# Channel products in float16 parts with column scales found on the chip

## The chip, the cores and the metric

The kernel runs on one core of a Trainium2 chip. A core has five engines with instruction queues of their own: TensorE (PE; its weight loads are listed apart as PEld), VectorE (DVE), ScalarE (ACT), GpSimd (POOL) and SyncE (SP, which here only starts transfers). Each takes its instructions in order and they wait for each other by semaphores. The metric is the device time of one execution in microseconds; less is better.

## What is computed

An encoder block for a sequence of 2048 tokens and one of 256, each token 1024 numbers in float32. One input projection feeds a short gated convolution (512 channels) and a latent attention with 8 heads; both are gated and joined by an output projection, and the result is normalised and added to the input.

```python
def _rmsnorm(x, g):
    xf = x.astype(jnp.float32)
    y = xf * lax.rsqrt(jnp.mean(xf * xf, axis=-1, keepdims=True) + NORM_EPS)
    return (y * g.astype(jnp.float32)).astype(x.dtype)

def _layer(x, norm_pre, w_in, conv_w, q_norm, w_uq, kv_norm, w_ukv, w_out, norm_post):
    hdn = _rmsnorm(x, norm_pre)
    proj = jnp.einsum('bsd,de->bse', hdn, w_in)
    u, b_gate, c_gate, z_conv, q_lat, kv_lat, k_pe, z_attn = jnp.split(proj, _split_points(), axis=-1)
    conv_out = b_gate * _short_conv(c_gate * u, conv_w) * jax.nn.silu(z_conv)
    ...
    attn_out = _attention(q_full, k_full, v) * jax.nn.silu(z_attn)
    mix = jnp.concatenate([conv_out, attn_out], axis=-1)
    out = jnp.einsum('bse,ed->bsd', mix, w_out)
    return x + _rmsnorm(out, norm_post)
```

The change is in the projection's columns u, b_gate, c_gate, z_conv and z_attn, five times 512 channels: 20 tiles of 128 channels.

## The kernel before

Float32 accuracy is made of three matmuls: each operand is cut into a rounded part hi and the rest lo, and `mm3` (L87) adds hi by hi, hi by lo and lo by hi in PSUM.

`phase1` (L103) works on the 2304 tokens as 6 chunks of 384 in two halves of three. For a chunk, `fetch_t` (L129) loads the transposed tokens into `xt` (one buffer, 1.5 MB), and `form` (L138) multiplies them by the norm's weights g_pre and cuts them into `hdn_hi` and `hdn_lo` in a rounded float32 type (F32R). `fetch_x` and `norm_x` (L144, L149) load 128 tokens at a time, and make their norms' factors (tile rc) with `rstd` (L96), a raising to the power -0.5 on GpSimd. `latents` (L176) makes the 672 columns of q_lat, kv_lat and k_pe of 128 tokens (tiles pq, pk); the weights wl are cut once. Nine such tiles make up a half.

`spread` (L166) turns a half's nine columns of factors into one row through TensorE and memory (r_s) and reads it back into all partitions (tile rb).

Then come the half's 20 tiles of channels. `load_w` (L231) fetches 512 KB of weights (tile w) and cuts them, ScalarE making whi, VectorE wlo. `etile` (L242) makes, for three chunks, 24 products each into PSUM (tile o; 72 products a tile of channels, 2880 in all), and multiplies by the tokens' row rb as it reads them: u into cu (e = 0), c_gate times cu (e = 1, with rb once more on GpSimd), b_gate into gt (e = 2), and silu of z into gt (e = 3), after which `conv` (L295) does the three taps. The last four tiles of a half (j = 4) are z_attn, stored to memory as gate. The weights of tile n + 1 are asked for just ahead of tile n.

From tile 24 on the preparation of the second phase (`Phase2.open`) is fed in between. After phase1 come the projections from the latents (L91 to L93 on k, v, q), attention with its order by hand, and the output projection. In `phase1` no order is written by hand: a scheduler places each instruction on its engine's queue by priority and expected readiness, and the queues then run in that order.

## Time and profile before

| | us |
|---|---|
| median of 3 runs (1690.73 to 1694.63) | 1692.76 |
| the profiled execution's own time | 1692.56 |
| its span | 1690.6 |
| TensorE busy in the span | 1647.5 (97%) |
| VectorE, ScalarE, GpSimd busy | 750.2, 581.6, 878.5 |

The profile is one execution. Busy time is from the start of an instruction to its recorded end; matmuls overlap each other by design, so what a matmul costs in a dense stretch is the time from its start to the next one's. The chain that ended last names 11% on TensorE, in the output projection: it reaches back only a short way, so the stages have to be read from tables by stretch and from the timeline.

### The profile page before, as it was taken

The page shows a single profiled execution, that of the slowest core. Times are in us where ns is not written, and L with a number is a line of the kernel's source. Part 1 is how long each engine was busy: PE and PEld are TensorE (multiplying, and loading weights), DVE is VectorE, ACT ScalarE, POOL GpSimd, SP SyncE. Part 2 cuts the span into 40 slices and gives each one's busy share as a digit, 9 for nine tenths or more (in the row PEclk, how much of TensorE's full clock was granted, in tenths as well). Part 3 has the DMA queues.
Part 4 walks back from the last instruction along what each step waited for, and adds up shares of the span by engine and source line. Part 5 has one row for each costly group of instructions (what it writes and reads, how often), then busy time and mean ns, then how long its engine had stood idle before and what let it go on. Part 6 is the DMA issues. An engine that isn't in the chain of part 4 may idle for free. (4 is left out here: it accounts for less than half of the span.)

```text
span 1690.6 us, 22364 instructions
## 1 busy us (share of the span) xinstructions
PE 1647.5 (97%) x8870; PEld 1115.8 (66%) x8870; DVE 750.2 (44%) x1125; ACT 581.6 (34%) x804; POOL 878.5 (52%) x637
## 2 busy tenths in 40 slices
PE   8999999999999999978999999999999999999998
PEld 8999999999999997556333333333333333378886
DVE  4333332423474222337556665666666666132122
ACT  7521111452222122411444444444444444512211
POOL 3321221033342112145788988989899898942222
PEclk9999999999999999989999999999999999999999
DMA  8921112364324116378011131113111210034443
GB/s 292 273 87 60 52 52 83 112 165 118 114 94 137 55 62 167 106 194 214 13 32 32 44 85 41 44 32 94 31 45 32 69 44 13 26 105 144 149 141 109
DMA packets 141741, 158.97 MB, mean 94 GB/s; under 512 B 33842, under 2 KB 118116, under 8 KB 141636
## 3 DMA queue, kind: packets, MB, share of 16 engines
q1 hardware_dynamic: 122916, 148.11, 29.3%
q10 hardware_dynamic: 18720, 9.44, 1.9%
q8 instruction: 69, 1.13, 0.3%
q14 instruction: 36, 0.29, 0.1%
HBM read 109.72 MB, written 41.89 MB: 90 GB/s over the span
## 5 line engine op out<-in xcount | busy, mean ns | idle before, releaser
L809 POOL TENSOR_TENSOR acc<-acc,p 128x1024 f32<-128x1024 f32 x224 | 527.9, 2357 | 60.6 <-ACT p L799 50.5
L753 DVE TENSOR_REDUCE mx<-m 128x1 f32<-128x512 f32 x512 | 337.7, 691 | 237.2 <-PE m L752 237.1
L799 ACT ACTIVATE p<-s,exps 128x1024 f32<-128x1024 f32 x256 | 271.4, 1111 | 348.2 <-PE s L794 348.2
L91 PE MATMUL o<-hdn_hi,whi 128*128 128x384 f32 x960 | 323.5, 337 | 0.0
L92 PE MATMUL o<-hdn_lo,whi 128*128 128x384 f32 x960 | 322.7, 336 | 0.0
L93 PE MATMUL o<-hdn_hi,wlo 128*128 128x384 f32 x960 | 322.6, 336 | 0.0
L789 PE MATMUL s<-q,k 128*128 128x512 f16 x1024 | 302.7, 381 | 1.0 <-ACT p L799 1.0
L920 PE MATMUL o<-p,v 128*64 128x512 f32 x1024 | 247.7, 605 | 0.0
L789 PEld LDWEIGHTS <-k 128*128 128x128 f16 x1024 | 90.7, 98 | 190.8 <-issue 101.4
L752 PE MATMUL m<-k,q 96*128 96x512 f16 x512 | 195.4, 382 | 14.4 <-DVE mx L753 8.7
L91 PEld LDWEIGHTS o<-hdn_hi,whi 128*128 128x128 f32 x960 | 180.5, 188 | 0.5
L92 PEld LDWEIGHTS o<-hdn_lo,whi 128*128 128x128 f32 x960 | 180.5, 188 | 0.0
L93 PEld LDWEIGHTS o<-hdn_hi,wlo 128*128 128x128 f32 x960 | 180.5, 188 | 0.0
L920 PEld LDWEIGHTS o<-p,v 128*64 128x64 f32 x1024 | 62.2, 136 | 127.5 <-issue 127.0
L959 PE MATMUL out<-wo,o_cut 128*128 128x512 f32 x576 | 140.4, 396 | 0.0
L959 PEld LDWEIGHTS out<-wo,o_cut 128*128 128x128 f32 x576 | 108.0, 188 | 27.7 <-issue 0.8
L948 POOL TENSOR_TENSOR o_cut<-o_raw,o_cut 128x1024 fp32r<-128x1024 f32 x17 | 40.8, 2399 | 118.3 <-ACT o_cut L945 118.3
L279 POOL TENSOR_TENSOR gt<-gt,z 128x384 f32<-128x384 f32 x24 | 28.7, 1197 | 141.1 <-ACT z L278 141.1
L236 ACT ACTIVATE whi<-w 128x1024 fp32r<-128x1024 f32 x40 | 42.2, 1058 | 172.8 <-PE o L92 159.6
L752 PEld LDWEIGHTS <-q 96*128 96x128 f16 x512 | 49.6, 97 | 63.9 <-issue 6.2
L967 DVE TENSOR_TENSOR yt<-out,g_post 128x1024 f32<-128x1024 f32 x18 | 22.0, 1224 | 150.7 <-ACT junko L966 141.7
L271 POOL TENSOR_TENSOR cu<-cu,rb 128x384 f32<-128x384 f32 (+2 forms) x28 | 27.5, 987 | 112.4 <-DVE cu L270 112.4
(230 smaller groups left out, 2016.4 us busy)
## 6 DMA issues: line engine op xcount, KB each, us to landing
w<-in_w_e_dram SPq DMA_DIRECT2D x40, 512.0 KB, 3.5
x<-in_x_dram SPq DMA_DIRECT2D x18, 512.0 KB, 6.8
o_raw<-mix_s SPq DMA_DIRECT2D x18, 512.0 KB, 4.8
o_raw<-in_x_dram SPq DMA_DIRECT2D x18, 512.0 KB, 5.6
out_dram<-yt SPq DMA_DIRECT2D x18, 512.0 KB, 6.2
q<-qn_s SPq DMA_DIRECT2D x64, 128.0 KB, 2.7
xt<-in_x_t_dram SPq DMA_DIRECT2D x5, 1536.0 KB, 8.3
k<-kn_s SPq DMA_DIRECT2D x12, 512.0 KB, 7.1
```

The source lines that it names most:

```text
L91: nc.tensor.matmul(out, sh, mh, start=first and i == 0, stop=False)
L92: nc.tensor.matmul(out, sh, ml, start=False, stop=False)
L93: nc.tensor.matmul(out, sl, mh, start=False, stop=last and i == n - 1)
L236: nc.scalar.activation(hi, w, AF.Copy)
L752: nc.tensor.matmul(m, q[:DQK, i, 2, b * P : (b + 1) * P], k[:DQK, i, 1, c * 512 : (c + 1) * 512], start=True, stop=True)
L753: nc.vector.reduce_max(mx[:, u, c : c + 1], m, axis=AX.X)
L789: nc.tensor.matmul(o, k[:, ki, x, ks], q[:, qi, x, :], start=x == 0, stop=False)
L799: nc.scalar.activation(p, o, AF.Exp, scale=g.exps[:, 0:1])
L809: nc.gpsimd.tensor_tensor(self.acc[key], self.acc[key], first, op=ALU.add)
L920: nc.tensor.matmul(self.o[n][i * DV : (i + 1) * DV], g.v[:, kt, h * DV : (h + 1) * DV], p[:, i * QB : (i + 1) * QB], start=kt == 0, stop=k ...
L948: eng.tensor_tensor(ml, m, f(mh), op=ALU.subtract)
L959: nc.tensor.matmul(o[:, w], mh[:, k, :], wk[k // 2][:, k % 2, w], start=k == 0 and wk is hi, stop=False)
```

## The change

The channels' products take float16 parts instead of F32R parts. For that both operands are scaled by powers of two. The tokens are multiplied by their norm's factor ahead of the products (`form_unit`: xt times rb, then cut into float16 unit_hi and unit_lo at 2^10), so the row rb is needed chunk by chunk, and `spread` runs six times. The weights are multiplied by g_pre, and a power of two for each column is found on the chip: squares, a sum over the eight rows of each partition (`load_w`), a sum over partitions by a matmul with ones, the power -0.5 of 128x128 numbers, the exponent alone, times 2^14 (`scale_w`); the weights are multiplied by it and cut into float16 w_hi and w_lo. `turn_scale` turns the scale's row into a column u by a matmul (tile wcol) and takes it back out when o is read. Weights are now asked for two tiles ahead and scaled one tile ahead, in the three gaps of `etile`. The tiles hdn have two buffers instead of three, and x two; four tiles of the second phase's preparation go from 768 to 704 columns.

```diff
-            xt = pw.tile([P, D], F32, tag="x", bufs=3, name=f"x{i}")
+            xt = pw.tile([P, D], F32, tag="x", bufs=2, name=f"x{i}")
...
-                    px.tile([P, 8, CH], F32R, tag="hdn_hi", bufs=3, name=f"hdn_hi{c}"),
+                    px.tile([P, 8, CH], F32R, tag="hdn_hi", bufs=2, name=f"hdn_hi{c}"),
...
+                unit[c] = [px.tile([P, 8, CH], F16, tag=f"unit_{w}", bufs=3, name=f"unit_{w}{c}") for w in ("hi", "lo")]
...
+        def form_unit(c, ks):
+
+            hi, lo = (t[:, ks] for t in unit[c])
+            src = turned[c][:, ks]
+            rb = scales[c][1].unsqueeze(1).to_broadcast([P, ks.stop - ks.start, CH])
+            nc.vector.tensor_tensor(src, src, rb, op=ALU.mult)
+            split(nc, hi, lo, src, X_UP)
...
-        def load_w(e, ident):
-            w = pb.tile([P, 8, P], F32, tag="w32", bufs=2, name=f"w{ident}")
-            nc.sync.dma_start(w, w_e[e])
-            hi = pb.tile([P, 8, P], F32R, tag="w_hi", bufs=2, name=f"whi{ident}")
-            lo = pb.tile([P, 8, P], F32R, tag="w_lo", bufs=2, name=f"wlo{ident}")
-            nc.scalar.activation(hi, w, AF.Copy)
-            nc.vector.tensor_tensor(lo, w, f(hi), op=ALU.subtract)
-            wq.append((hi, lo))
+        def load_w(n):
...
+            w = pb.tile([P, 8, P], F32, tag="w32", bufs=2, name=f"w{n}")
+            nc.sync.dma_start(w, w_e[4 * j + e])
+            nc.gpsimd.tensor_tensor(w, w, g_pre.unsqueeze(2).to_broadcast([P, 8, P]), op=ALU.mult)
+            sq = pb.tile([P, 8, P], BF16, tag="w_sq", bufs=1, name=f"wsq{n}")
+            nc.scalar.activation(sq, w, AF.Square)
+            ssq = pb.tile([P, P], F32, tag="w_ssq", bufs=1, name=f"wssq{n}")
+            nc.vector.reduce_sum(ssq, sq.rearrange("p k e -> p e k"), axis=AX.X)
+            short = pb.tile([P, P], BF16, tag="w_short", bufs=1, name=f"wshort{n}")
+            nc.gpsimd.tensor_copy(short, ssq)
+            wq[n] = (w, short)
+
+        def scale_w(n):
...
+            w, short = wq[n]
+            acc = ps.tile([P, 3, P], F32, tag="tl", name=f"wacc{n}")
+            nc.tensor.matmul(acc[:, 0], ones, short, start=True, stop=True)
+            p = pb.tile([P, P], F32, tag="w_p", bufs=1, name=f"wp{n}")
+            nc.vector.tensor_scalar(p, acc[:, 0], 1e-36, None, op0=ALU.add)
+            nc.gpsimd.tensor_tensor(p, p, g.mhalf[:, :1].to_broadcast([P, P]), op=ALU.pow)
+            power(nc, p)
+            nc.gpsimd.tensor_scalar(p, p, WE_UP, None, op0=ALU.mult)
+            nc.vector.tensor_tensor(w, w, p.unsqueeze(1).to_broadcast([P, 8, P]), op=ALU.mult)
+            hi, lo = (pb.tile([P, 8, P], F16, tag=f"w_{a}", bufs=2, name=f"w{a}{n}") for a in ("hi", "lo"))
+            split(nc, hi, lo, w)
+            wq[n] = (hi, lo, p)
+
+        def turn_scale(n):
...
+            hi, lo, p = wq[n]
+            acc = ps.tile([P, 3, P], F32, tag="tl", name=f"wcol{n}")[:, 0, :2]
+            nc.tensor.matmul(acc, p[:1], one[:1], start=True, stop=True)
+            col, u = (pb.tile([P, 1], F32, tag=f"w_{a}", bufs=2, name=f"w{a}{n}") for a in ("c", "u"))
+            nc.vector.tensor_scalar(col, acc[:, :1], X_UP, None, op0=ALU.mult)
+            unpower(nc, u, col)
+            wq[n] = (hi, lo, u)
...
-                hi, lo = hdn[c]
+                hi, lo = unit[c]
...
+                between(ci)
...
-                        nc.vector.tensor_tensor(cs, o[:, a:b], r[:, a:b], op=ALU.mult)
+                        nc.scalar.activation(cs, o[:, a:b], AF.Copy, scale=u)
                     elif e == 1:
-                        nc.vector.tensor_tensor(cs, o[:, a:b], cs, op=ALU.mult)
-                        nc.gpsimd.tensor_tensor(cs, cs, r[:, a:b], op=ALU.mult)
+                        nc.vector.scalar_tensor_tensor(cs, o[:, a:b], u, cs, op0=ALU.mult, op1=ALU.mult)
...
+        spread(0)
+        form_unit(0, slice(0, 8))
         fetch_t(1, slice(0, 8))
...
+                    if i and i % 3 == 0:
+                        form_unit(c, slice(0, 8))
+                        if ahead:
+                            fetch_t(c + 1, slice(0, 8))
+                    if i == 5 or i == 6:
+                        load_w(i - 5)
+                    if i == 7:
+                        scale_w(0)
+                        turn_scale(0)
...
-                    etile(n)
+
+                    def between(ci):
+                        if ci == 0:
+                            load_w(n + 2)
+                        else:
+                            (scale_w, turn_scale)[ci - 1](n + 1)
+
+                    etile(n, between)
```

How the scheduler places this on TensorE is seen where tile 1 ends and tile 2 begins. Before, with whi2 and wlo2 the weights' parts of tile 2, o2_0 its sums for the half's first chunk, and tk8 a turned k_pe:

```order
L93 MATMUL o1_2_1076<-hdn_hi2_438,wlo1_931 128x384
L223 MATMUL tk8_1104<-ident_69,kpl8_903 32x128
L91 MATMUL o2_0_1115<-hdn_hi0_103,whi2_1018 128x384
L92 MATMUL o2_0_1115<-hdn_lo0_104,whi2_1018 128x384
L93 MATMUL o2_0_1115<-hdn_hi0_103,wlo2_1019 128x384
```

With the change, on the same engine and at the same place (wp2 is the scale of tile 2, wacc3 the sums of squares for tile 3):

```order
L95 MATMUL o1_2_1179<-unit_hi2_533,wlo1_1064 128x384
L286 MATMUL wcol2_1204<-one_w_104,wp2_1168 128x2
L239 MATMUL tk8_1214<-ident_69,kpl8_982 32x128
L93 LDWEIGHTS whi2_1174
L93 MATMUL o2_0_1219<-unit_hi0_109,whi2_1174 128x384
L94 LDWEIGHTS whi2_1174
L94 MATMUL o2_0_1219<-unit_lo0_110,whi2_1174 128x384
...
L269 MATMUL wacc3_1279<-wshort3_1138,ones_w_102 128x128
...
L95 MATMUL o2_0_1219<-unit_hi0_109,wlo2_1175 128x384
```

The matmul wcol2, which reads the scale of tile 2, now stands ahead of all of tile 2's products, and the sum for tile 3 stands after four of them; in tile 3 the sum for tile 4 stands behind 48 products. Of the 39 tiles that are followed by another, 13 have that sum after 4 products, 23 after 48 to 50, one after 72; ahead of tile 32 the sum and the turned scale of tile 33 come as well.

On GpSimd, around tiles 2 and 3. Before (cu, gt and cy are the convolution's tiles, z3_0 the gate of tile 3's first chunk):

```order
L271 TENSOR_TENSOR cu_99<-cu_99,rb0_162 128x384 x2
L292 COPY carry_101<-cu_99 128x2
L279 TENSOR_TENSOR gt_100<-gt_100,z3_0_1224 128x384
L313 TENSOR_TENSOR cy0_0_0_1228<-cy0_0_0_1228,gt_100 128x383
L279 TENSOR_TENSOR gt_100<-gt_100,z3_1_1259 128x384
```

With the change, where L272 is the power, L274 the multiply by 2^14, L254 the multiply by g_pre and L260 the narrowing of the sums:

```order
L272 TENSOR_TENSOR wp2_1168<-wp2_1168,mhalf_76 128x128
L274 TENSOR_SCALAR wp2_1168<-wp2_1168 128x128
L341 COPY carry_101<-cu_99 128x2
L272 TENSOR_TENSOR wp3_1281<-wp3_1281,mhalf_76 128x128
L274 TENSOR_SCALAR wp3_1281<-wp3_1281 128x128
L254 TENSOR_TENSOR w4_1244<-w4_1244,g_pre_95 128x1024
L260 CAST wshort4_1251<-wssq4_1249 128x128
L254 TENSOR_TENSOR w5_1351<-w5_1351,g_pre_95 128x1024
L328 TENSOR_TENSOR gt_100<-gt_100,z3_0_1360 128x384
L362 TENSOR_TENSOR cy0_0_0_1363<-cy0_0_0_1363,gt_100 128x383
L260 CAST wshort5_1358<-wssq5_1356 128x128
L272 TENSOR_TENSOR wp4_1396<-wp4_1396,mhalf_76 128x128
```

Each tile has put a power and three other steps into GpSimd's queue, and the multiplies for the convolution stand between them.

## Rows read from the trace of the kernel before

**Rows 1.** The page, whole span: engine, busy us, share, instructions.
```profile
PE 1647.5 (97%) x8870; PEld 1115.8 (66%) x8870; DVE 750.2 (44%) x1125; ACT 581.6 (34%) x804; POOL 878.5 (52%) x637
```

**Rows 2.** Table by stretch: length, busy (count) of each engine, granted clock, DMA.
```profile
75.50:325.00 249.50, 249.50 (x1443) 249.34 (x1441) 81.57 (x113) 49.45 (x79) 50.03 (x65) 1.00 0.22 74
325.00:392.00 67.00, 67.00 (x440) 66.80 (x438) 18.95 (x34) 35.68 (x92) 17.61 (x50) 1.00 0.57 152
392.00:645.50 253.50, 252.74 (x1488) 251.42 (x1488) 106.76 (x198) 54.64 (x88) 72.89 (x80) 1.00 0.31 96
```

**Rows 3.** Timeline of TensorE, keys and values: start, length, instruction.
```profile
648.64 0.27 PE L93 MATMUL k<-lt_kv,uk_lo 128*128 128x256 f16 x1
648.75 0.38 PE L91 MATMUL v<-uv_hi,lt_kv 128*128 128x512 f16 x1
648.97 0.38 PE L92 MATMUL v<-uv_lo,lt_kv 128*128 128x512 f16 x1
649.18 0.38 PE L93 MATMUL v<-uv_hi,lt_kv 128*128 128x512 f16 x1
```

**Rows 4.** Groups by line and shape on GpSimd: busy us, mean ns, idle before.
```profile
L488 POOL TENSOR_TENSOR c<-c,mhalf 128x1 f32<-128x1 f32 x1 | 0.6, 551 | 0.8 <-DVE c L487 0.8
L100 POOL TENSOR_TENSOR rl<-rl,mhalf 128x2 f32<-128x2 f32 x18 | 13.1, 726 | 1.5
L477 POOL TENSOR_TENSOR uv_col<-ssq,mhalf 128x4 f32<-128x4 f32 x1 | 1.0, 1039 | 0.9 <-DVE ssq L454 0.9
L472 POOL TENSOR_TENSOR rho<-rho,mhalf 128x5 f32<-128x5 f32 x1 | 1.2, 1167 | 0.6 <-DVE rho L471 0.6
L467 POOL TENSOR_TENSOR b_r<-b,mhalf 128x10 f32<-128x10 f32 x1 | 2.0, 1964 | 5.3 <-DVE b L466 5.3
```

**Rows 5.** Timelines of GpSimd and of VectorE around one power.
```profile
457.25 1.96 POOL L467 TENSOR_TENSOR b_r<-b,mhalf 128x10 f32<-128x10 f32 x1 [5.27 <-DVE b L466]
...
459.25 0.17 DVE L468 TENSOR_TENSOR b<-b,b_r 128x10 f32<-128x10 f32 x1 [0.68 <-POOL b_r L467]
```

**Rows 6.** Groups by line and shape on three engines.
```profile
L237 DVE TENSOR_TENSOR wlo<-w,whi 128x1024 fp32r<-128x1024 f32 x40 | 52.0, 1301 | 11.0 <-ACT whi L236 10.7 <-DMA lat_s<-lt 0.4
L236 ACT ACTIVATE whi<-w 128x1024 fp32r<-128x1024 f32 x40 | 42.2, 1058 | 172.8 <-PE o L92 159.6 <-issue 11.1 <-DMA w<-in_w_e_dram 2.1
L507 DVE TENSOR_SCALAR diag<-ident,qa 128x128 bf16<-128x128 f32 x4 | 0.9, 277 | 0.0
L271 POOL TENSOR_TENSOR cu<-cu,rb 128x128 f32<-128x128 f32 x4 | 1.6, 412 | 9.8 <-DVE cu L270 9.8
```

**Rows 7.** Table by stretch, then TensorE's timeline, at its two longest late waits.
```profile
738.00:740.00 2.00, 0.00 (x0) 0.00 (x0) 0.00 (x0) 0.00 (x0) 0.00 (x0) 0.50 1.13 358
...
752.00:754.00 2.00, 1.44 (x6) 0.87 (x7) 0.69 (x1) 0.00 (x0) 0.00 (x0) 0.50 0.55 152
...
740.79 0.37 PE L91 MATMUL qr<-lt_q,uq_hi 128*128 128x256 f16 x1 [6.24 <-DMA lt_q<-lat_s]
...
743.37 0.42 PE L93 MATMUL qr<-lt_q,uq_lo 128*128 128x256 f16 x1
...
743.78 0.27 PE L92 MATMUL qr<-lt_q,uq_hi 128*128 128x256 f16 x1
...
752.56 0.58 PE L752 MATMUL m<-k,q 96*128 96x512 f16 x1 [5.12 <-DMA q<-qr_s]
...
757.53 0.27 PE L91 MATMUL qr<-lt_q,uq_hi 128*128 128x256 f16 x1
```

**Rows 8.** Timelines of GpSimd, SP and VectorE; then a DMA issue with its median us.
```profile
23.02 0.49 POOL L163 TENSOR_SCALAR rn<-rc 128x1 f32<-128x1 f32 x2
...
76.12 0.35 SPq L173 DMA_DIRECT2D r_s<-rr  x1
...
83.42 0.56 DVE L268 TENSOR_TENSOR cu<-o,rb 128x384 f32<-128x384 f32 x1 [3.79 <-DMA rb<-r_s]
...
xt<-in_x_t_dram SPq DMA_DIRECT2D x5, 1536.0 KB, 8.3
```

More of the change, by code (lines that the diff above doesn't have):

```diff
@@ L40 @@
 LAT_UP = 2.0**11
+X_UP = 2.0**10
+WE_UP = 2.0**14
 W_UP = 2.0**4
@@ L120, in phase1 @@
         carry = pb.tile([P, 4, 3], F32, name="carry", bufs=1)
+        ones = pb.tile([P, P], BF16, name="ones_w", bufs=1)
+        nc.gpsimd.memset(ones, 1.0)
+        one = pb.tile([P, 2], F32, name="one_w", bufs=1)
+        nc.gpsimd.memset(one, 1.0)
         hdn = {}
         turned = {}
+        unit = {}
         xns = {}
@@ L342, in extra @@
                     norm_x(i + 3)
-                    form(c + 1, (range(4), range(4, 8), ())[i % 3])
-                    if i % 3 == 2 and c + 2 < 3 * hf + 3:
-                        fetch_t(c + 2, slice(0, 8))
+                    form(c + 1, ((), range(4), range(4, 8))[i % 3])
+                    if i % 3 == 2:
+                        spread(c + 1)
                 for tiles in ([[0, 1], [2]] if c == 0 else [[3 * c + t] for t in range(3)]):
@@ L380, in phase1 @@
                         norm_x(i)
+                if hf == 0 and j == 4:
+                    spread(3)
+                    form(3, range(8))
             if hf == 1:
@@ L430, in open @@
             nc.gpsimd.tensor_scalar(gs[:, at : at + n], gw[:, at : at + n], DOWN * num**0.5, None, op0=ALU.mult)
[L431 removed]
+        stage = lambda name, n: pst.tile([P, 8, P], F32, tag="w32", bufs=2, name=name).rearrange("p k e -> p (k e)")[:, :n]
         for name, src, kt, n, at in srcs:
@@ L981, in tile_encoder @@
     g.kpe = dram.tile([ROPE, T], F32, name="kpe_s")
-    g.r = dram.tile([2, HALF], F32, name="r_s")
+    g.r = dram.tile([6, CH], F32, name="r_s")
     g.gate = dram.tile([CW, T], F32, name="gate_s")
```

70 lines of the change are left out of this document (32 added, 38 removed).

## The prediction

> **What bounds the kernel now.** I read the page first: TensorE is busy 1647.5 of 1690.6 us [rows 1]. The table by stages then says where the change falls. The channels' products (tile o) fill two stretches, 75.5 to 325 and 392 to 645.5 us, with the latents of the second half between them; in all three TensorE has no gap to speak of, and GpSimd works 50 of 249.5 and 73 of 253.5 us [rows 2]. So each of the 2880 products costs its start-to-start time, and any other engine that one tile of products waits for costs its whole wait. The first stretch holds half of the products: 249.5 / 1440 = 0.173 us each, with the weight load busy all through (249.34 of 249.50) [rows 2]. One tile of 128 channels is 72 products, 12.5 us; there are 40.
>
> **What the change removes.** In float16, matmuls of 256 columns start 0.11 us apart and those of 512 columns 0.215 us [rows 3]; a line between them gives 0.163 us for 384 columns. The gain is 2880 x 0.0103 = 30 us, and a tile becomes 72 x 0.163 = 11.7 us. The evacuations lose their multiply by the norm's row and GpSimd loses that of cu; both lay beside the products and are worth nothing here.
>
> **What it adds on the path: the scale of each tile.** Per tile, GpSimd multiplies the weights by g_pre, ScalarE squares, VectorE sums, GpSimd narrows; a matmul with ones sums over partitions; VectorE adds a constant; GpSimd raises 128x128 numbers to -0.5; VectorE masks; GpSimd multiplies by a constant. Only then can VectorE scale the weights, ScalarE make hi and VectorE lo. TensorE's row wcol(n+1), which turns the scale into a column, stands ahead of tile n+1's first product and reads the finished scale, so everything behind it on TensorE waits.
>
> The pow has five sizes in the trace: 551 ns for 1 column, 726 for 2, 1039 for 4, 1167 for 5, 1964 for 10 [rows 4]. From 1 to 10 columns that is (1964 - 551) / 9 = 157 ns a column; from 2 to 4 it is 157, from 5 to 10 it is 159. It is no artefact of GpSimd's records: the 10-column pow starts at 457.25 and takes 1.96, and VectorE, which waits for it, starts at 459.25 [rows 5]. At 128 columns: 0.55 + 127 x 0.157 = **20.5 us**. The nearest row in size, the other way, is a plain 128x128 multiply on GpSimd, 0.41 us [rows 6]. I take 20.5, since the rows of the same operation lie on a line, and keep 0.41 as the lower end.
>
> A rule speaks against so long a pow: the Trainium skill (GPSIMD Engine Reference, 3.1 Elementwise — side-by-side cycle accounting) puts GpSimd's tensor_tensor add at about 2.6 cycles an element. If that held for pow, 128 columns at its 1.2 GHz would take about 0.3 us beside the dispatch (an estimate from that page). The trace disagrees for pow: 157 ns a column is some 60 times as much.
>
> The other links, from rows: VectorE on 128x1024 1.30, ScalarE on 128x1024 1.06, VectorE on 128x128 0.28, GpSimd on 128x128 0.41 [rows 6]; the mask 0.17 like VectorE's other small steps [rows 5]; the sum's matmul 0.27 like a short float16 matmul's length [rows 3]; 0.1 for each handover. From "scale ready" to hi is 2.6 us and to lo 4.0. From the sum's matmul to the next scale is 0.65 + 20.5 + 0.65 = 21.8 us.
>
> TensorE's clock: around the waits of 6.24 and 5.12 us the granted clock reads 0.50, that is 1.2 GHz, and matmuls of 256 columns are 0.42 us long instead of 0.27 until 743.78 and 757.53, 3.0 and 5.0 us after the first one started [rows 7]. At half the pace half of that is lost, 1.5 to 2.5 us; I take 1.9 for each tile that starts after a long wait.
>
> The order decides how much of 21.8 us is covered. Of the 39 links from tile n to n+1, 13 have the sum for n+1 after 4 products of tile n, 23 after 48 to 50, one (25) after all 72; before tile 32 the scale of 33 is made as well, and then both tiles run.
> - Early (13): hi 2.6, four products at the slow clock 1.3, then 21.8: **25.7 us**. TensorE needs 4.0 + 11.4 + 1.9 = 17.3 of them and stands the rest.
> - Late (23): lo 4.0, 46 products 7.5, clock 1.9, then 21.8: **35.2 us**.
> - The odd ones: 39.1 (25), 21.8 (32 to 33), 45.7 (33 to 34).
>
> Sum: 13 x 25.7 + 23 x 35.2 + 106.6 = 1250; in about seven tiles with z a multiply of gt stands on GpSimd between pow and its scaling (3 x 0.41 [rows 6]), +8; the last tile 17.3. Together 1275 us. GpSimd's other new work (the 128x1024 multiply by g_pre, the narrowing) is ordered behind a pow or while the products run, about 13 us after a scale, just ahead of the late sum at 13.4; it is hidden, and costs 1 to 2 us a link where it isn't. On SP the weights of tile n+2 wait for the buffer that tile n's split reads, and some for convolution stores queued ahead; the pow leaves them time.
>
> **The latents.** A tile of them is 67 / 9 = 7.4 us [rows 2]. The tokens' tile has one buffer, and xt(1) may be fetched only after form_unit(0), which needs the norms' row through memory. On SP the fetch now also stands behind the second chunk's r_s and rb, a transpose, kpe_s and lat_s. In before that row took 7.3 us from its store (76.12) to its reader (83.42) [rows 8]. The three norms are done at 23.5 us [rows 8]; with the transposition behind the matmuls of tile 2 already queued, near 26, the row is there at 33, three passes over 128x3072 at three times 1.30, 1.06 and 1.30 = 11, the fetch 8.3 [rows 8]: chunk 1 starts near 53.5 instead of 75.5 - 6 x 7.4 = 31. **+23 us** (10 to 30). Chunk 2's fetch falls just behind the latents of chunk 1, and in the second half the next fetch has a chunk's 22 us; I take 2 us there.
>
> **Sum.** Scale 0 is begun when tile 8's latents (7.4 us) are still to come: 75.5 + 23 - 8 + 22 = 113 us. The rest of these latents, at the slow clock, puts the first link 6 us later: 119. Then 1275, the second half's latents 67 + 2 [rows 2], less 6 since they cover one tile's preparation: 1457 us for the end of the products. In before it is 645.5. What follows is untouched: + 811.5. The profiled execution's own time is 1692.56 us (span 1690.6 and 2 us around it; the median shown is 0.2 us more): 1692.6 + 811.5 = **2504**.
>
> **Rivals.**
> 1. Pow has a cheap path for wide tiles, 0.41 us instead of 20.5 [rows 6]. For: nothing in the trace is wider than 10 columns. Against: five sizes on one line. TensorE stays warm; late links still lack lo by 0.65 + 0.45 + 0.65 + 4.0 - 3.9 (the third chunk's products) = some 1.5 us with part of it covered by two products: 26 x 1.5 = 39, less 30, plus 25 for the start: 1725. The rate on the Trainium skill's page (GPSIMD Engine Reference, 3.1) would end here too. Chance 0.04.
> 2. Not slower: the products' pace is all that ends last. Place: TensorE's row wcol. It decides where the link from sum to lo fits under what is left of a tile, 3.9 us late or 11.1 us early; at 20.5 us it fits neither, at 0.41 the early ones. It needs rival 1 and hidden splits and the start covered too: 1692.6 - 30 = 1663. Chance 0.03.
> 3. Pow wide is half as dear (several columns in a pass): 2504 - 40 x 10 = 2100. Chance 0.04.
> 4. The waits stack: GpSimd's narrowing of the sums, with the multiplies of gt and cy queued ahead, comes after the sum's turn and delays each pow by 5 us or more: 2504 + 40 x 5 = 2700. For: GpSimd is in order and full. Against: it has 8 us of room early. Chance 0.05.
> That float16 products gain nothing (the change doesn't do what it says) is +30 us, inside the range.
>
> **How the numbers follow.** Forecast 0.84, rivals 0.04, 0.03, 0.04, 0.05. Pow within 5% is 40 us, the clock's 1.5 to 2.5 is 20, the start -13 to +7, links 0 to 2 us longer is +80: 2430 to 2610 about the sum, and to 2380 and 2650 so that with part of rivals 3 and 4 no more than 2 in 10 is out. Faster 0.03; within 0.2% (about what a measurement of this kernel tells from no change) 0.02; slower 0.95.
>
> **What would show it.** Right: pow at 128x128 near 20.5 us x40 on GpSimd; TensorE's longest waits before wcol, each for GpSimd's scale, 8 us and 18 us in turn; granted clock clearly under 1 in the stretch; the products' stretch some 2.5 times as long; products 0.163 us apart between waits; from the keys' stage on, nothing changed. Wrong: a pow of a few us; waits of wcol for something else (a DMA of weights, VectorE); or a first chunk without a wait of some 20 us.

## The result and the profile after

The changed kernel takes 2627.77 us (median of 4 runs, 2624.74 to 2636.43), the kernel before 1692.95 beside it: a ratio of 1.553, 95% interval 1.549 to 1.557. The forecast was 2504 us, range 2380 to 2650. The direction, the place and the mechanism were right. The sum was 124 us short, and the account of the prediction below says where these 124 lie.

The page, whole span of 2627.9 us, answers to [rows 1]:

```profile
PE 1742.7 (66%) x8994; PEld 950.1 (36%) x8994; DVE 928.8 (35%) x1361; ACT 664.8 (25%) x902; POOL 1802.5 (69%) x771
```

TensorE is busy for 66% of the span instead of 97%, and GpSimd has become the busiest engine. What TensorE waited for (its line and tile, the releaser, us in total, times, the longest):

```profile
PE wcol L286 <- POOL wp L274: 679.1, 39, 25.8
PE o L93 <- ACT whi L70: 86.7, 36, 3.5
PE row L187 <- POOL rc L102: 22.2, 4, 13.9
PE wcol L286 <- POOL cu L338: 20.7, 1, 20.7
PE pq L93 <- ACT hdn_hi L150: 15.5, 3, 12.0
```

The turned scale waits 40 times, once for each tile (the fourth line is the same wait, put down to a small step that ended last), for 700 us together. The second line is the way from the scale to whi, still on the path once a wait has begun. The third and fifth are the later start of the latents.

GpSimd's groups by line and shape (busy us, mean ns of one, idle before) give the reason, beside the five sizes of [rows 4]:

```profile
L272 POOL TENSOR_TENSOR wp<-wp,mhalf 128x128 f32<-128x128 f32 x40 | 830.1, 20752 | 53.7 <-DVE wp L271 40.8 <-DVE wu L79 9.3 <-DVE wu L84 1.6
L254 POOL TENSOR_TENSOR w<-w,g_pre 128x1024 f32<-128x1024 f32 x40 | 76.9, 1922 | 61.0 <-DMA w<-in_w_e_dram 59.8 <-DVE hdn_lo L151 1.0
L274 POOL TENSOR_SCALAR wp<-wp 128x128 f32<-128x128 f32 x40 | 25.5, 637 | 11.2 <-DVE wp L79 10.6 <-DVE wu L79 0.5
```

The table by stretch (length, busy us and count of PE, PEld, DVE, ACT, POOL, granted clock, DMA share, GB/s) answers to [rows 2]; the stretches are the start, the first half's tiles, the second half's latents with the tile ahead of them, the second half's tiles (with the first 21 us of the keys' stage), and all the rest:

```profile
31.00:75.50 44.50, 17.52 (x95) 16.09 (x94) 22.28 (x20) 20.52 (x40) 13.10 (x23) 0.65 0.48 135
128.00:772.00 644.00, 285.34 (x1467) 161.91 (x1466) 150.91 (x220) 80.23 (x123) 483.87 (x129) 0.70 0.09 30
772.00:895.00 123.00, 91.66 (x543) 82.36 (x544) 47.49 (x57) 50.16 (x107) 52.09 (x58) 0.85 0.36 100
895.00:1605.00 710.00, 306.77 (x1670) 174.14 (x1669) 174.60 (x304) 93.70 (x138) 503.23 (x139) 0.70 0.12 37
1605.00:2627.90 1022.90, 989.11 (x4915) 464.73 (x4912) 506.16 (x722) 382.51 (x420) 710.84 (x369) 0.99 0.27 80
```

In both stretches of tiles TensorE works under half the time, GpSimd about three quarters, and the granted clock is 0.70, a mean over both levels: the first products after a wait run at 1.2 GHz (0.32 us apart, for 3 us in the last tile), the later ones at 2.4 GHz (0.1625 apart). The keys' stage starts at 1584.2 us; from there to the end are 1043.7 us, before 1044.5: everything that was gained or lost lies ahead of it.

### The profile page after: what moved, and what is told of

Read it like the earlier page. It is cut to its first block, busy times and chain, and to the rows that moved or that the text cites. A ratio compares the mean times of both kernels' runs of the same rounds, so it can differ in the third digit from the quotient of the medians.

```text
span 2627.9 us, 23093 instructions
## 1 busy us (share of the span) xinstructions
PE 1742.7 (66%) x8994; PEld 950.1 (36%) x8994; DVE 928.8 (35%) x1361; ACT 664.8 (25%) x902; POOL 1802.5 (69%) x771
## 5 line engine op out<-in xcount | busy, mean ns | idle before, releaser
L272 POOL TENSOR_TENSOR wp<-wp,mhalf 128x128 f32<-128x128 f32 x40 | 830.1, 20752 | 53.7 <-DVE wp L271 40.8
L871 POOL TENSOR_TENSOR acc<-acc,p 128x1024 f32<-128x1024 f32 x224 | 527.5, 2355 | 61.0 <-ACT p L861 51.1
L286 PE MATMUL wcol<-one_w,wp 1*128 1x2 f32 x80 | 23.3, 358 | 699.8 <-POOL wp L274 679.1
L93 PE MATMUL o<-unit_hi,whi 128*128 128x384 f16 x960 | 349.0, 364 | 86.7 <-ACT whi L70 86.7
L94 PE MATMUL o<-unit_lo,whi 128*128 128x384 f16 x960 | 344.8, 359 | 0.0
L95 PE MATMUL o<-unit_hi,wlo 128*128 128x384 f16 x960 | 332.1, 351 | 7.0 <-DVE wlo L71 6.2
L286 PEld LDWEIGHTS wcol<-one_w,wp 1*128 1x128 f32 x80 | 19.8, 306 | 717.9 <-POOL wp L274 696.8
L70 ACT ACTIVATE whi<-w 128x1024 f16<-128x1024 f32 x40 | 42.3, 1056 | 894.9 <-DVE w L275 894.9
L93 PEld LDWEIGHTS <-whi 128*128 128x128 f16 x960 | 102.3, 107 | 166.2 <-ACT whi L70 91.8
L95 PEld LDWEIGHTS <-wlo 128*128 128x128 f16 x960 | 100.0, 104 | 93.3 <-DVE wlo L71 21.5
L94 PEld LDWEIGHTS <-whi 128*128 128x128 f16 x960 | 102.1, 106 | 73.8 <-issue 25.2
L254 POOL TENSOR_TENSOR w<-w,g_pre 128x1024 f32<-128x1024 f32 x40 | 76.9, 1922 | 61.0 <-DMA w<-in_w_e_dram 59.8
```

Source lines behind the costliest of these rows:

```text
L93: nc.tensor.matmul(out, sh, mh, start=first and i == 0, stop=False)
L94: nc.tensor.matmul(out, sh, ml, start=False, stop=False)
L95: nc.tensor.matmul(out, sl, mh, start=False, stop=last and i == n - 1)
L254: nc.gpsimd.tensor_tensor(w, w, g_pre.unsqueeze(2).to_broadcast([P, 8, P]), op=ALU.mult)
L272: nc.gpsimd.tensor_tensor(p, p, g.mhalf[:, :1].to_broadcast([P, P]), op=ALU.pow)
L871: nc.gpsimd.tensor_tensor(self.acc[key], self.acc[key], first, op=ALU.add)
```

## The experiments

All are edits of the changed kernel. Each was run beside the kernel before on the same chip; where a ratio is given it is to that.

### One word: a multiply in the pow's place

```diff
-            nc.gpsimd.tensor_tensor(p, p, g.mhalf[:, :1].to_broadcast([P, P]), op=ALU.pow)
+            nc.gpsimd.tensor_tensor(p, p, g.mhalf[:, :1].to_broadcast([P, P]), op=ALU.mult)
```

> One word changes: GpSimd multiplies the 128x128 sums by -0.5 where it raised them to -0.5, at the same place in an order that is the same on every engine. So each column's power of two is taken from the sum of squares itself and not from its inverse root. Theory (the pow's length is the loss): the step falls from 20.75 to about 0.41 us, the ten thousandfold repeated wait of TensorE's row wcol for GpSimd goes, early links are bound by the products (11.7 us), late ones by 48 products (7.8) + sum to scale (some 4.3 as measured after the change, less the pow) + scale to lo (3.6) = 13.0 to 15.4 us; with 29 us for chunk 1's later start and 15 for the second half's: 1740 to 1780. Rival A (the waits of the other links stack as much as the pow: narrowing, gt and cy ahead on GpSimd): above 1850. Rival B (GpSimd is slow for any 128x128 step with a broadcast operand): stays near 2600.

(The "ten thousandfold" is a slip of the pen; there are 40 such waits.) Measured: 1827.36 us, ratio 1.081 (1.079 to 1.083). The step, and what TensorE then waited for:

```profile
L272 POOL TENSOR_TENSOR wp<-wp,mhalf 128x128 f32<-128x128 f32 x40 | 16.2, 405 | 48.0 <-DVE wp L271 34.3 <-DVE wu L79 9.3 <-DVE wu L84 2.1
```

```profile
PE o L93 <- ACT whi L70: 27.7, 18, 3.0
PE row L187 <- POOL rc L102: 23.6, 4, 13.8
PE wcol L286 <- POOL wp L274: 20.2, 11, 3.8
```

The traces show the same order on every engine, and the operand is spread over the columns in the same way, so 2627.8 - 1827.4 = 800 us come of the pow alone, and rival B falls. The step is shorter by 20.35 us, 40 times, which makes 814: nearly all of its length was time of the kernel. (The 800 hold the clock as well, which falls less without the long waits: 0.97 granted from 111 to 380 us, the first half's tiles.) But 1827 is above the 1740 to 1780 that I expected without it, though below rival A's 1850: the rest of the change costs more than I had counted.

### The pow on half of the columns

```diff
-            nc.gpsimd.tensor_tensor(p, p, g.mhalf[:, :1].to_broadcast([P, P]), op=ALU.pow)
+            half = P // 2
+            nc.gpsimd.tensor_tensor(p[:, :half], p[:, :half], g.mhalf[:, :1].to_broadcast([P, half]), op=ALU.pow)
+            nc.gpsimd.tensor_tensor(p[:, half:], p[:, half:], g.mhalf[:, :1].to_broadcast([P, half]), op=ALU.mult)
```

> The pow takes 64 of the 128 columns, a multiply by -0.5 the other 64 (whose power of two so comes from the sum itself); TensorE's order is the same. Theory (157 ns a column, whole length on the path): pow 0.55 + 63 x 0.157 = 10.4 us, multiply some 0.3; each of 40 scales comes 20.75 - 10.8 = 9.9 us sooner and every link is still longer than the 11.7 us of the products, so the time falls by 40 x 9.9 = 396 to about 2230, give or take 30. Rival (a cost of the instruction and not of its columns, or a floor of another wait): the pow stays above 15 us, or the time falls by clearly less than 380.

Measured: 2231.74 us (one run). The two halves:

```profile
L273 POOL TENSOR_TENSOR wp<-wp,mhalf 128x64 f32<-128x64 f32 x40 | 422.2, 10554 | 55.8 <-DVE wp L271 42.9 <-DVE wu L79 9.3 <-DVE wu L84 1.6
...
L274 POOL TENSOR_TENSOR wp<-wp,mhalf 128x64 f32<-128x64 f32 x40 | 11.7, 292 | 0.0
```

10.55 us for 64 columns, 20.75 for 128: 159 ns a column, the slope of [rows 4]. The chain became 20.75 - 10.85 = 9.9 us shorter, and the time fell by 396, 40 times that. So the price goes by columns, and as long as a link is longer than its products, each us of it is a us of the kernel.

### The same pow, one number to a partition

The 128 sums are equal in all partitions. Here they are laid one to a partition, so that the pow is of 128x1, and go back to a row by a matmul with a diagonal:

```diff
-            nc.tensor.matmul(acc[:, 0], ones, short, start=True, stop=True)
+            nc.tensor.matmul(acc[:, 0, :2], short, ones[:, :2], start=True, stop=True)
...
+            nc.gpsimd.tensor_tensor(p, p, g.mhalf[:, :1], op=ALU.pow)
             power(nc, p)
...
+            nc.vector.tensor_scalar(diag, g.ident, p, WE_UP, op0=ALU.mult, op1=ALU.mult)
...
+            nc.tensor.matmul(row, ones, diag, start=True, stop=True)
```

> The same pow on GpSimd, but of the 128 sums laid one to a partition (128x1, by a matmul with the sums' tile as weights and ones as moving part) instead of 128 equal rows (128x128); the scale goes back to a row by a matmul of ones with a diagonal, and the turned scale falls away. Nothing is left out. Theory (157 ns a column, not a cost of the instruction): the pow takes 0.55 us, the chain from sum to scale some 3.5 us with two handovers to GpSimd, and the time is near that of the run with a multiply in the pow's place, 1827: 1780 to 1830. Rival (pow is dear by the number of its values, 128 here): about 16384 / 128 = 1/128 of 20.2 above its start, the same 0.55 to 0.7, so the two agree; a pow of over 2 us would contradict both. A second matmul that waits for GpSimd in the middle of a tile could cost TensorE 2 to 4 us a tile: then above 1850.

Measured: 1838.75 us, ratio 1.088 (1.086 to 1.089), 9 us over the expected span: TensorE now stands before the second matmul (wrow, 29 times, 54 us together). The pow itself:

```profile
L272 POOL TENSOR_TENSOR wp<-wp,mhalf 128x1 f32<-128x1 f32 x40 | 22.3, 557 | 43.6 <-DVE wp L271 42.3 <-DVE wu L85 1.3
```

The same 128 numbers cost 0.56 us as one column and 20.75 us as 128 columns (128 equal rows of 128): what is paid for is columns.

### No pow and no GpSimd between sum and scale

```diff
-            nc.gpsimd.tensor_tensor(p, p, g.mhalf[:, :1].to_broadcast([P, P]), op=ALU.pow)
-            power(nc, p)
-            nc.gpsimd.tensor_scalar(p, p, WE_UP, None, op0=ALU.mult)
+            m = 0x7F000000
+            nc.vector.tensor_scalar(p.bitcast(I32), p.bitcast(I32), m, m, op0=ALU.bitwise_and, op1=ALU.bitwise_xor)
+            nc.vector.tensor_scalar(p.bitcast(I32), p.bitcast(I32), 1, None, op0=ALU.logical_shift_right)
+            nc.vector.tensor_scalar(p, p, 2.0**63 * WE_UP, None, op0=ALU.mult)
```

> The pow, the mask and the multiply by 2^14 on GpSimd go; VectorE makes the same kind of power of two from the sum's exponent by three 128x128 steps on its bits (and with xor, a shift by one, a multiply). Nothing is left out; TensorE's order is nearly that of the change. Theory (the pow was the loss, and in the run with a multiply in its place the rest of the waits was GpSimd's queue between sum and scale): sum to scale becomes 0.3 + 4 x 0.3 + handovers, about 1.8 us, so late links are 7.8 + 1.8 + 3.6 = 13.2 us and early ones 11.7: 22 x 1.5 = 33 us above the run with the fixed scale (1725), some 1760 (1745 to 1780). Rival (what is left is GpSimd's multiply by the norm's weights and its narrowing, which stay): like the run with the multiply, 1810 to 1830.

Measured: 1829.30 us, ratio 1.082 (1.080 to 1.084), the same as with the multiply. So the theory that GpSimd's queue between sum and scale held the rest fell; the outcome was the rival's number, but this run can't tell whether by the rival's reason. TensorE's waits in it are still waits for the search: 26.1 us before wcol for VectorE's scale (12 times), 27.4 before o for the cut weights, 9.1 before the sum. Its stretches are the first half's tiles, the latents between and the second half's tiles:

```profile
113.00:383.30 270.30, 254.15 (x1504) 148.26 (x1501) 158.39 (x262) 85.05 (x125) 81.44 (x93) 0.97 0.22 74
383.30:465.15 81.85, 72.19 (x445) 70.82 (x445) 39.92 (x45) 43.09 (x93) 28.79 (x49) 0.92 0.49 134
465.15:788.00 322.85, 269.87 (x1543) 153.84 (x1541) 185.22 (x338) 89.24 (x137) 93.15 (x102) 0.90 0.21 69
```

### No search at all

The weights are cut at a fixed 2^14; squares, sums, pow and wcol go.

```diff
...
-            split(nc, hi, lo, w)
-            wq[n] = (hi, lo, p)
+            split(nc, hi, lo, w, WE_UP)
+            wq[n] = (hi, lo, 1.0 / (X_UP * WE_UP))
```

> The search for the scale is left out: no squares, sums, pow or wcol; the weights are multiplied by the norm's weights and cut into float16 parts at a fixed 2^14, and the outputs are read with one constant. Float16 products, six rows of norms and the tokens' one buffer stay. Theory: products at 0.1625 us give back 30 us; chunk 1 still starts at about 60 instead of 31 us and the second half's latents still take some 82 instead of 67 us, and nothing else waits: 1692.6 - 30 + 29 + 15 = 1707 (1695 to 1720). Rival A (float16 products gain nothing): 1735. Rival B (the later start is hidden or was caused by the scale's work): 1665 to 1680. Rival C (the weights' multiply on GpSimd and their buffers hold TensorE): waits before o for whi of over 2 us a tile, above 1780.

Measured: 1724.97 us, ratio 1.019 (1.017 to 1.022); expected 1707. The same stretches, with the latents from chunk 1 on ahead of them:

```profile
60.10:111.83 51.73, 48.41 (x294) 47.60 (x294) 26.56 (x29) 27.40 (x58) 13.67 (x26) 0.93 0.43 111
111.83:346.10 234.27, 234.27 (x1446) 140.88 (x1443) 59.47 (x67) 60.51 (x106) 71.30 (x74) 1.00 0.26 83
346.10:431.60 85.50, 73.73 (x444) 71.95 (x443) 39.80 (x42) 44.30 (x96) 28.43 (x51) 0.90 0.45 129
431.60:680.70 249.10, 241.01 (x1486) 143.37 (x1483) 87.74 (x147) 63.83 (x116) 87.81 (x80) 0.98 0.31 96
```

The float16 products give what was counted: 234.27 us for 1440 instead of 249.5 [rows 2], 0.1627 each. In the second half 4 of 15 us are left, since 8 us of waits for the second phase's preparation stand in it, where the kernel before had 0.7. Against these 19.6 us, the first product starts 36.3 us later than before (111.8 instead of 75.5) and the second half's latents take 18.5 more (85.5 instead of 67). Net 35, measured 33.9. And the tiles with a search but no pow, the run above, are 270.3 - 234.3 = 36 and 322.9 - 249.1 = 74 us longer.

Taken away in this order, the 935 us of the change are thus: 800 the pow, 102 the rest of the search (1827.4 - 1725.0), 34 the later latents less the products' gain. Another order would share them out otherwise, since waits cover each other.

### Where the late links come from: the sum first, then a third buffer

```diff
-                        else:
-                            (scale_w, turn_scale)[ci - 1](n + 1)
-
+                        elif ci == 2:
+                            turn_scale(n + 1)
+
+                    scale_w(n + 1)
                     etile(n, between)
```

> The pow stays; the sum and the pow of tile n+1 are written ahead of tile n's products instead of behind 48 of them, so on TensorE the sum stands at the head of the tile (34 of 39). Theory (late links cost the 46 products that stand ahead of their sum): every link becomes sum to scale, 0.3 + 0.4 + 20.75 + 1.4 = 22.9, plus what GpSimd does between two pows (the multiply by the norm's weights 1.92, the narrowing 0.38 and in some tiles gt and cy), 23 to 26 us; 22 late links fall by some 13 us, 12 early ones by 2, two odd ones by some 30 together: 2628 - 340 = 2290 (2250 to 2370). Rival (the late links are long because steps on GpSimd and VectorE stack and not because of TensorE's order): falls by under 100, to above 2500.

Measured: 2657.43 us (one run): nothing was won, 30 us lost. The pow is there, the sum does stand first (TensorE runs it 0.57 us after the scale in 24 of 39 links), and nearly every link is 34 to 37 us long, where 26 to 28 and 34 to 44 had taken turns. GpSimd around one link:

```profile
514.48 0.54 POOL L274 TENSOR_SCALAR wp<-wp 128x128 f32<-128x128 f32 x1 [0.35 <-DVE wu L79]
522.16 1.90 POOL L254 TENSOR_TENSOR w<-w,g_pre 128x1024 f32<-128x1024 f32 x1 [7.14 <-DMA w<-in_w_e_dram]
527.25 0.29 POOL L260 CAST wshort<-wssq 128x128 bf16<-128x128 f32 x1 [3.20 <-DVE wc L288]
527.50 20.75 POOL L272 TENSOR_TENSOR wp<-wp,mhalf 128x128 f32<-128x128 f32 x1
```

The sum for the next tile ran on TensorE at 515.6; its pow starts at 527.5. Ahead of it in GpSimd's order stand the multiply and the narrowing of the tile after that, whose weights can be fetched only when VectorE has cut the last ones out of the same buffer (the cutting ends at 518.7). VectorE's order has it too: the addition behind the sum starts at 527.07, right behind the reduction of the tile after. The wait had moved from TensorE's order to that of two others.

A second run keeps this order, gives the weights a third buffer, and makes the tokens' units from hdn, with the norm's weights in them, so that GpSimd's multiply of w falls away. For room, lp has three buffers instead of four, and the squares share the tile junk:

```diff
-            w = pb.tile([P, 8, P], F32, tag="w32", bufs=2, name=f"w{n}")
+            w = pb.tile([P, 8, P], F32, tag="w32", bufs=3, name=f"w{n}")
...
-            nc.gpsimd.tensor_tensor(w, w, g_pre.unsqueeze(2).to_broadcast([P, 8, P]), op=ALU.mult)
```

> The pow stays; the sum stands at the head of the tile as in the run with the sum first, but the weights have three buffers, and the norm's weights are in the tokens (made from hdn, as in the run with all three), so that on GpSimd only the narrowing stands ahead of a pow. Theory (in the run with the sum first every pow stood behind the work on the next weights, which waited for the buffer that the last scaling releases): nothing is waited for but sum, pow and scale: 0.3 + 0.4 + 20.75 + 1.4 and some gt and cy, 23.5 to 25 us a link; 38 x 24.5 + 100 for the half's change, scale 0 some 15 us sooner: 2170 (2130 to 2260). Rival (the links are long for another reason, such as cold clock or the stores queued ahead of the weights): above 2450.

Measured: 2437.2 us (one run), 220 less than the run before it (17 of them ahead of the first product, at 119.4 instead of 136.9 us) and 267 above what I expected, just below the rival's 2450. Of its 39 links 15 are 25.6 to 26.3 us: there the addition waits only for VectorE to scale and cut the last weights, which stand ahead of it in its order:

```profile
442.43 1.23 DVE L71 TENSOR_TENSOR wlo<-w,whi 128x1024 f16<-128x1024 f32 x1 [1.18 <-ACT whi L70]
443.57 0.15 DVE L289 TENSOR_SCALAR wc<-wcol 128x1 f32<-128x1 f32 x1
443.64 0.28 DVE L272 TENSOR_SCALAR wp<-wacc 128x128 f32<-128x128 f32 x1
```

The others, but for the one across the second half's latents, are still 28 to 37, their pow begun 6 to 16 us after the scale. Buffer and multiply were part of the cause; which one, and what holds the others, these two runs don't separate. In both, the pow itself stays the larger part of every link.

### The start of the latents

Again without the search, the units are made from hdn_hi plus hdn_lo, so that xt is free as early as before, and the norms' row stands behind a chunk's first latents:

```diff
+                nc.gpsimd.tensor_tensor(src, f(hdn[c][0][:, k]), f(hdn[c][1][:, k]), op=ALU.add)
+                nc.vector.tensor_tensor(src, src, rb, op=ALU.mult)
+                split(nc, hi, lo, src, X_UP)
...
+        fetch_t(1, slice(0, 8))
         spread(0)
-        form_unit(0, slice(0, 8))
-        fetch_t(1, slice(0, 8))
```

> As the run with the fixed scale (the search for the scale is left out), but the float16 tokens are made from hdn_hi plus hdn_lo in a small buffer and no longer from xt, so that the next chunk's tokens are fetched as soon as hdn is cut, as in the kernel before; the transposed norms' row of a chunk stands behind that chunk's first latents; the norm's weights then are in the tokens and not multiplied into w. Theory (the later latents are the wait for the one tokens' buffer and the row ahead of them on TensorE): chunk 1 starts near 31 instead of 60 us, the second half's latents take 67 to 72 instead of 85 us, and the float16 products' gain is left: 1725 - 36 - 15 = 1675 (1660 to 1690). Rival A (two instead of three buffers of hdn and of x hold the latents in any case): 1700 to 1715. Rival B (GpSimd's 48 additions or the later row hold the first tile of products): chunk 1 early, but the first product not before 95 us.

Measured: 1702.31 us, ratio 1.0075 (1.0054 to 1.0096). Chunk 1 starts at 32.7 us as meant, the first product at 94.6, the second half's latents take 78.7: 23 of 55 us came back, and the outcome fell to rival A's number. TensorE still waited 17.6 us for the norms' row. With x in three buffers again and the row behind the second latents:

> As the run with the fixed scale and early tokens (the search for the scale is left out), with three buffers of x again as in the kernel before, and the row of a chunk's norms behind its second latents instead of its first. Theory (what is left of the later start there, first product at 94.6 instead of 75.5 us and 78.7 instead of 67 us for the second half's latents, is TensorE standing before the norms' row, 17.6 us in four places, and x in two buffers): most of the 31 us comes back while the products still give some 19 to 30: 1702 - 25 = 1677 (1665 to 1692), at or a little below the kernel before. Rival (two buffers of hdn, or GpSimd's 48 additions, hold the latents): stays at 1695 to 1705.

Measured: 1713.65 us, ratio 1.014 (1.012 to 1.016): slower, a miss. No wait for rc is among the longer ones now and the latents between the halves take 68.4 us, but the units now come after the products are due:

```profile
110.19 0.48 PE L93 MATMUL o<-unit_hi,whi 128*128 128x384 f16 x1 [3.76 <-ACT unit_hi L73]
```

So the last chunk's row and units were made one tile sooner:

```diff
-                    if i % 3 == 1 and c % 3:
+                    if i % 3 == (0, 1, 0)[c % 3] and c % 3:
                         spread(c)
-                    if i % 3 == 2:
+                    if i % 3 == (1, 2, 1)[c % 3]:
                         form_unit(c, slice(0, 8))
```

> As the run with three buffers of x (the search for the scale is left out), but the norms' row and the float16 tokens of the last chunk of a half are made one tile of latents sooner, so that the first products don't wait for unit. Theory (there the wait only moved from the row to the units, 12.2 + 6.2 us before o): these 18 us and the cold clock after them go, the latents keep their 68 us in the second half: 1713.7 - 20 = 1694 (1685 to 1702), no different from the kernel before, because hdn in two buffers still costs some 8 us at the start and phase 2's preparation some 7 us of waits. Rival (the row again stands before its norms): 1700 to 1715.

Measured: 1691.57 us (12 runs), ratio 1.0011 (1.0001 to 1.0021): within 0.2% of the kernel before, as expected. It is the best version found, without the search, and it does not beat the kernel before.

### What the search costs TensorE itself

All three improvements with the search: the scale by VectorE, the units from hdn, the sum behind 24 products.

```diff
                         if ci == 0:
+                            scale_w(n + 1)
+                        elif ci == 1:
                             load_w(n + 2)
-                        else:
-                            (scale_w, turn_scale)[ci - 1](n + 1)
+                            turn_scale(n + 1)
```

> Nothing is left out: the scale by VectorE's steps on the exponent, the float16 tokens from hdn, and the sum for tile n+1 behind 24 products of tile n instead of 48, the loading of tile n+2 behind 48. Theory: sum to lo is 1.8 + 3.6 us and starts 3.9 us into a tile of 11.7, so no link is longer than its products; with the start as in the run with the fixed scale and early tokens (some 1675) and a few us for squares, sums and the first scale: 1680 (1665 to 1700), within 1% of the kernel before on the lower side. Rival (VectorE, which now carries sums, scale, splits and tokens, becomes late): waits of o for wlo or whi of over 1 us a tile, 1720 or more.

Measured: 1761.01 us, ratio 1.042 (1.039 to 1.044), far below the change, still slower than before and on the rival's side: TensorE waits before wcol for VectorE's scale, 28 us in 8 times. Of the 59 us over the run with early tokens, 16 lie in the first half's tiles (254.2 instead of 238.4) and 40 in the second's (286.2 instead of 245.75). One of these waits, 7.7 us, stands in the first half's tiles and seven, 20.2 us, in the second's. Even where no wait stands, a tile takes longer than in the run with early tokens. The next run puts two matmuls of the search's kind into the tiles of the run with early tokens, with nothing to wait for and no reader:

```diff
+            nc.tensor.matmul(acc[:, 0], ones, short, start=True, stop=True)
...
+            nc.tensor.matmul(acc, row[:1], one[:1], start=True, stop=True)
```

> As the run with the fixed scale and early tokens (the search is left out), with two matmuls a tile put into TensorE's order that read constants and whose results nobody reads: one like the sum over partitions (128x128 bfloat16) and one like the turned scale (1x128 by 2 columns, float32), behind 48 of the tile's 72 products. Theory (the search costs TensorE its own time even where nothing waits: in the run with all three the products' pace over 115 to 350 us was 12.3 us a tile and in the run with the fixed scale and early tokens 11.9): 0.4 to 0.6 us a tile, 40 times: 1702 + 16 to 24 = 1718 to 1726. Rival (short matmuls slip into the products' weight loads and cost nothing): 1702 within 4 us.

Measured: 1718.88 us, ratio 1.017 (1.016 to 1.019): 16.6 us more, at the lower edge of what was expected. The products alone (tile o) on TensorE in the 200 us from 120 to 320, where nothing waits: of the run with early tokens, of this one and of the run with all three:

```profile
120.00:320.00 200.00, 200.00 (x1232) 1.00 0.22 73
```

```profile
120.00:320.00 200.00, 195.25 (x1186) 1.00 0.21 69
```

```profile
120.00:320.00 200.00, 196.00 (x1185) 1.00 0.21 75
```

From the first product of a tile to the first of the next are 11.70 us without the two matmuls, 12.17 with them and 12.17 with the search. The timeline of the run with the two matmuls shows what each takes:

```profile
165.73 0.33 PE L95 MATMUL o<-unit_hi,wlo 128*128 128x384 f16 x1
165.89 0.22 PE L277 MATMUL wacc<-w_short,ones_w 128*128 128x128 bf16 x1
166.04 0.38 PE L279 MATMUL wcol<-one_w,w_p 1*128 1x2 f32 x2
166.35 0.34 PE L93 MATMUL o<-unit_hi,whi 128*128 128x384 f16 x1
```

From product to product are 0.62 us instead of 0.16. The sum takes 0.15 of the difference and the turned scale, two float32 matmuls in the trace, 0.31. So 0.46 us a tile, 18 us in all, are the search's own time on TensorE in this form, and in a dense row of products they lie on the path: of the 30 us that float16 gives, 12 would be left to a perfect order. In the run with all three they make up some 9 us of each half. With the waits that is all of the first half's 16 us, and 29 of the second's 40; the other 11 were not separated (the granted clock there is 0.96, in the run with early tokens 0.99).

## Why the prediction was right, and which terms were off

**The pow.** Predicted 20.5 us from five sizes on a line, measured 20.75; TensorE's longest waits are where they were put, before wcol, once a tile; in the first half they take turns as foreseen, but last some 10 and 22 us instead of 8 and 18. Rivals 1 to 3 fall with that row. The rate on the Trainium skill's page (GPSIMD Engine Reference, 3.1), which spoke against it, is that of an add and does not hold for this operation: 159 ns a column, some 70 times that rate (an estimate from the page's 2.6 cycles at 1.2 GHz) and not 60 as the prediction says. Rival 1's price was wrong, though: with a step of 0.41 us the kernel takes 1827, not 1725.

**The links.** Between the first scale (ready at 127.1) and the last (1568.4) lie 1441 us; the sum had 1327. It breaks up by kind:
- Early, 12 without the first: 27.15 us in the mean instead of 25.7, +17. From the sum to the pow are 1.41 us instead of 0.65, from its end to the scale 0.94 instead of 0.65, the pow itself is 0.25 longer. The mask takes 0.45 and not 0.17, the multiply by 2^14 0.64 and not 0.41 (means of the 40); I had taken the first from a shape of 10 columns.
- Late, 22: 38.4 instead of 35.2, +71, the largest term. The sum comes when predicted (13.75 us after the scale, 13.4 foreseen). What was mis-sized is behind it: from the sum to the pow 2.54 instead of 0.65, from its end to the scale 1.37 instead of 0.65. Of the 1.9 us too many before the pow, 1.3 lie ahead of VectorE's addition (1.66 after the sum instead of 0.37) and 0.6 between it and the pow (0.88 instead of 0.28). The larger part is thus VectorE's order, which the prediction did not have: in nine of the 22 links the addition starts 1.9 to 7.1 us after the sum, behind steps of the convolution, the sums of the next weights' squares or the second phase's preparation. Here the sum ran at 174.24:

```profile
177.35 0.61 DVE L321 SCALAR_TENSOR_TENSOR cu<-o,wu,cu 128x384 f32<-128x384 f32 x1
177.88 0.28 DVE L271 TENSOR_SCALAR wp<-wacc 128x128 f32<-128x128 f32 x1
```

  In four links it is GpSimd's order, rival 4's mechanism: 2.3 to 3.5 us from the addition to the pow, where that rival asked for 5 or more in every link. I had written "hidden" for it. One such link, on GpSimd:

```profile
235.17 1.90 POOL L254 TENSOR_TENSOR w<-w,g_pre 128x1024 f32<-128x1024 f32 x1 [0.97 <-DMA w<-in_w_e_dram]
242.78 0.99 POOL L328 TENSOR_TENSOR gt<-gt,z 128x384 f32<-128x384 f32 x1 [5.71 <-ACT z L327]
243.85 1.00 POOL L362 TENSOR_TENSOR cy<-cy,gt 128x383 f32<-128x383 f32 x1
244.79 0.29 POOL L260 CAST wshort<-wssq 128x128 bf16<-128x128 f32 x1
245.04 20.75 POOL L272 TENSOR_TENSOR wp<-wp,mhalf 128x128 f32<-128x128 f32 x1
265.76 0.99 POOL L328 TENSOR_TENSOR gt<-gt,z 128x384 f32<-128x384 f32 x1
266.92 0.83 POOL L274 TENSOR_SCALAR wp<-wp 128x128 f32<-128x128 f32 x1 [0.17 <-DVE wp L79]
```

  The addition started at 241.55, so this pow could have begun at 241.9; gt, cy and the narrowing hold it until 245.04, and another gt stands between it and its scaling. I had allowed 8 us for gt in all.
- The odd ones: 48.9 (25), 24.2 (32 to 33), 45.2 (33 to 34) instead of 39.1, 21.8, 45.7, +12; the link across the second half's latents 118.2 instead of 98, +20.

Taken together: 17 + 71 + 12 + 20, less the 8 for gt, and 2 for the first link: 114.

**That the late links' length is the sum's place** on TensorE was right for this order, but not the whole of it: with the sum first, the links stay at 35, because the next weights' work stands ahead of the pow in two other queues. The trace of before could not show it; the order on GpSimd and VectorE could.

**The start.** Chunk 1 started at 60.3 us, not 53.5 (the terms named there, 33 + 11 + 8.3, add up to 52.3), and the first scale was ready at 127.1, not 113. The norms' row came at 37.05 instead of 33, and the three passes were shorter than counted (3.36, 2.76, 3.36). What was missing is a wait between them. ScalarE's, VectorE's and GpSimd's rows there:

```profile
37.05 3.36 DVE L158 TENSOR_TENSOR xt<-xt,rb 128x3072 f32<-128x3072 f32 x1 [1.36 <-DMA rb<-r_s]
```

```profile
37.07 3.77 POOL L102 TENSOR_TENSOR rc<-rc,mhalf 128x1 f32<-128x1 f32 x1
```

```profile
42.91 0.58 ACT L73 ACTIVATE lp<-pq,rl 128x384 f16<-128x384 f32 x1 [5.18 <-POOL rl L220]
...
44.78 2.76 ACT L73 ACTIVATE unit_hi<-xt 128x3072 f16<-128x3072 f32 x1
```

While VectorE multiplies the tokens, a one-column pow on GpSimd, 0.57 us elsewhere, takes 3.77; the latents' factors behind it come late, ScalarE stands 5.2 us for them, and the units stand behind that in its order, 4.4 us after the tokens were ready. That is chunk 1's 7 of the 14 us. The rest: its first tile of latents takes 9.7 us instead of 7.4 (granted clock 0.74), the first of chunk 2 takes 12.0 (TensorE stands 2.6 before the norms' row), and the first scale takes 23 instead of 22. The second half's latents, for which I added 2 us, take 18.5 more in the run without a search; part of that is the norms' row, which stands ahead of the latents on TensorE and comes late.

**The products and the rest.** 0.163 us in float16 was right (0.1627), the last tile 15.8 instead of 17.3 us, and the stages behind it unchanged, 1043.7 against 1044.5. In that tile the slow clock cost 1.6 us (3.15 us at half the pace), where 1.9 had been taken. The gain of 30 us was never whole: 8 us of waits in the second half's tiles took part of it, and 18 us of the search's own matmuls lie on TensorE wherever no wait covers them, a term that the sum did not have (in the changed kernel every tile has such a wait).

So the forecast held in direction and size because the pow was priced from its own rows. It missed by 124: 114 in the links and 14 before the first scale, less 1.5 in the last tile and some rest. That the time still lies in the range, 22 us below its upper end, is in part luck. For longer links the working allowed 80 us, and 114 came; it is also 18 us above the 2610 that the working names for its own terms (added up as they stand there, they reach 2651). What held it was room left for rivals, and the largest wait in it, VectorE's order, was not among them.

## To carry to other kernels

Price an operation from rows of that operation, over several sizes, before it is put 40 times into the chain that another engine waits for: a line through 1 to 10 columns gave the time at 128 within 1.5%. Lay the numbers so that the dear operation sees few columns. And before a faster product is paid for with a search, count what the search itself takes on the bounding engine, and look through every in-order queue between its links, not only the one that waits.

## What the runs showed of the hardware that was not expected

GpSimd and VectorE can hold each other up. The one-column pow above is one case. Another is the weights' scaling on VectorE, 1.23 us alone, when GpSimd's multiply by g_pre begins just ahead of it:

```profile
226.43 2.91 DVE L275 TENSOR_TENSOR w<-w,wp 128x1024 f32<-128x1024 f32 x1 [0.67 <-POOL wp L274]
```

```profile
226.37 1.90 POOL L254 TENSOR_TENSOR w<-w,g_pre 128x1024 f32<-128x1024 f32 x1
```

GpSimd's step ends at 228.27 and VectorE's at 229.34, 1.07 us later: nearly all of the second ran after the first, not beside it. The Trainium skill (Trainium Architecture — The Big Picture, What this means for kernel authors) says that the two engines share a port pair under an exclusive lock and don't split its bandwidth; these rows agree, both ways round. The long pow does not: while it runs from 245.04 to 265.79, a step of VectorE that reads two tiles takes no longer than elsewhere, 0.62 us, and so do the three others of its size that start well inside a pow:

```profile
247.47 0.62 DVE L359 SCALAR_TENSOR_TENSOR cy<-cu,cw,cy 128x384 f32<-128x384 f32 x1 [5.64 <-ACT cy L358]
```

So the long pow is paid by what waits for it, and not by VectorE's steps beside it.

A step of 128x128 on bits, 0.23 us undisturbed, is 0.45 in the mean of the 40 masks and 1.69 at the longest; in the run with all three one takes 2.04. The pow varies hardly at all: 20.74 to 20.92 us over 40.
